# Hybrid mLSTM / attention / gMLP block: which queue starts the projection's stores and the ne rows' spread

## The chip, the cores and the metric

The kernel runs on one core of one Trainium2 chip. The core has five engines, each with a queue of its own that works in order: TensorE (PE; its weight loads are PEld), VectorE (DVE), ScalarE (ACT), GpSimd (POOL) and SyncE (SP). A transfer (DMA) is begun by an instruction in one engine's queue and then runs on the core's 16 DMA engines. The metric is device microseconds of one execution, as the median of several runs; less is better.

## The reference

One layer of a decoder trunk over x (2048 positions, 1024 channels), all in float32. What matters here:

```python
h = rms_norm(x, g_mix) * (1 + scale1) + shift1        # shift, scale, gate from silu(c) @ W_ada + b_ada
p = h @ w_in                                          # one projection for all head groups
y_attn  = forgetting_attention(rms_norm(q_a), rms_norm(k_a), v_a, f_a + b)   # 8 heads x 64
y_mlstm = sigmoid(o_m) * rms_norm(mlstm_chunkwise(q_m, k_m, v_m, i_m, f_m))  # 4 heads x 64
y_sgu   = spatial_gating(gelu(u_s), gelu(v_s))                               # 4 groups x 64
x = x + gate1 * (concat(y_attn, y_mlstm, y_sgu) @ w_out)
x = x + gate2 * conv_ffn(rms_norm(x) * (1 + scale2) + shift2)   # up, causal conv of width 3, SwiGLU, down
```

The mLSTM is a matrix memory with gates in log space. Within a chunk, the weight of source s for target t is exp(a[s] + ne[t]) for s <= t, where a holds one number for each source and head, and ne (the negated running maximum, less the cumulated log gate) one for each target and head.

## The kernel before

Matmuls are exact to about float32: each operand is split into a high and a low part (types F32R), and `mm3` (L53 to L56) makes three products. The work goes through the core in stages: a start that loads x and the first adaptive weights; the projection (here up to about 818 us); attention; the output projection with the second norm; the up projection with the convolution; and the down projection.

**The projection.** `steps` walks over two halves of the sequence and, in each, over twelve column blocks of `w_in` in this order: km with the gates, qm, vm, om, vs, us, then k, v and q of attention, twice. `w_block` loads one block of weights ahead (tile wst, L564), ACT casts its high part (L569) and DVE makes the low part (L570). `natural` makes, for each of eight tiles of 128 positions, 24 matmuls into one of three PSUM banks (`acc`), and a `use_...` function empties the bank and sends the result to DRAM:

- `use_km` (L602): ACT copies, then the tile goes to km_d (L605). `do_qm` (L609): ACT scales, then qm_d (L619). `use_vm` and `use_om` do likewise, but what they send was last written by DVE or POOL.
- `spatial` (L661): four tiles of 128 positions together; ACT copies the transposed result, then yt_d (L679).
- `use_qk` (L692): ACT squares the bank (tile ev, L694), DVE sums, POOL takes the root (L132), DVE scales into qn (L700), which frees the bank. Four tiles later `turn` transposes qn on PE, ACT makes the high part qhi (L710), DVE the low part qlo (L711), and both are sent to q_d or k_d (L713). qhi and qlo share three buffers.

**Beside it.** `mod_sum` makes the rest of the adaptive vectors on DVE (L422, L424) from tiles wa of 256 KB that are loaded through four buffers (L414); `columns_or_row` sends the two gates' rows to gt_d (L468).

**The mLSTM** runs as a background generator, `mlstm(qi)`, for each 512 positions, a piece of which is put between two tiles of the projection. It writes four rows ne to DRAM (ne_d, L799). For each of four chunks of 128 positions, `raw` transposes k on PE, copies it on ACT (kT, L836), and loads into tile M1 (two buffers) the chunk's four ne rows, spread over all 128 partitions by the transfer itself (L838: 512 pieces of 512 bytes, 256 KB, read from the same 2 KB of DRAM). POOL adds the causal mask (L839). `decay` turns M1 into weights with four exponentials on ACT (L845). Then PE makes the scores, DVE multiplies them by M1 (sc, L868), which frees M1's buffer, and the state is brought forward. At the end ACT copies the transposed result and it goes to yt_d (L933).

**Order.** Each engine's queue is in order. The order within a queue isn't that of the program text: a planner (the list scheduler of the tile framework) plays the program through with modelled durations and puts each instruction, transfers included, into its engine's queue when its inputs are ready and its buffers free; among ready ones the earlier in the program goes first. Waits are put in afterwards. Before the change every transfer is begun by SP, which does nothing else.

Of the kernel before, what the change touches and what calls it, by code (L numbers as in the profile page):

```python
# [17 lines left out]
P = 128  # L18
# [6 lines left out]
TB = 512  # L25
# [8 lines left out]
def trunk(  # L34
# [6 lines left out]
    nc = tc.nc  # L41
    V, A, G, T = nc.vector, nc.scalar, nc.gpsimd, nc.tensor
    dma = nc.sync.dma_start
    x, out = x[0], out[0]
    w_ada, w_in, w_out, w_up, w_down = w_ada[0], w_in[0], w_out[0], w_up[0], w_down[0]

    def bc(ap, axis, n):
        u = ap.unsqueeze(axis)
        shape = list(u.shape)
        shape[axis] = n  # L50
        return u.broadcast_to(shape)

    def mm3(ps, lh, ll, rh, rl, start, stop, resume=False):  # L53
        T.matmul(ps, lh, rh, start=start, stop=False, skip_group_check=resume)  # L54
        T.matmul(ps, lh, rl, start=False, stop=False, skip_group_check=resume)  # L55
        T.matmul(ps, ll, rh, start=False, stop=stop, skip_group_check=resume)  # L56
# [9 lines left out]
    ne_d = dr.tile([4, S], F32, name="ne_d")  # L66
    qm_d = dr.tile([2, P, S], F32, name="qm_d")
    km_d = dr.tile([S, 256], F32, name="km_d")
    vm_d = dr.tile([S, 256], F32, name="vm_d")
    om_d = dr.tile([S, 256], F32, name="om_d")  # L70
    yt_d = dr.tile([D, S], F32, name="yt_d")
    y2_d = dr.tile([512, S], F32, name="y2_d")
    x2_d = dr.tile([S, D], F32, name="x2_d")
    gt_d = dr.tile([2, D], F32, name="gt_d")
# [56 lines left out]
    def rsqrt(t, n):  # L131
        G.tensor_tensor(t, t, nhalf[:, 0:1].broadcast_to([P, n]) if n > 8 else nhalf[:, :n], op=ALU.pow)  # L132
# [239 lines left out]
    def acc_ps():  # L372
        n_acc[0] += 1
        return pp.tile([P, 512], F32, name="acc", tag="acc2" if n_acc[0] % 3 == 0 and n_accs[0] == 3 else "acc")

    def tr_ps():
        return pp.tile([P, 512], F32, name="trp", tag="trp")

    def misc_ps():
        return pp.tile([P, 512], F32, name="mp", tag="mp")  # L380

    def mps():
        return pp.tile([P, 512], F32, name="mps", tag="mps")
# [77 lines left out]
    def columns_or_row(acc, col):  # L461
        kind, half = col // 1024, (col % 1024) // 512
        ps = misc_ps()
        if kind in (2, 5):
            T.matmul(ps, ones, acc, start=True, stop=True)
            gr = pool.tile([1, 512], F32, name="gr", tag="t2k")
            A.copy(gr, ps[0:1, :])
            dma(gt_d[kind // 3 : kind // 3 + 1, half * 512 : half * 512 + 512], gr)  # L468
        else:
            for j in range(4):  # L470
                T.matmul(ps[:, j : j + 1], acc[:, j * P : (j + 1) * P], ones[:, 0:1], start=True, stop=True)
            sl = slice(half * 4, half * 4 + 4)
            if kind == 3:
                V.tensor_copy(sh2[:, sl], ps[:, 0:4])
            else:
                V.scalar_tensor_tensor(
                    a2[:, sl], ps[:, 0:4], 1.0, gf[:, half * 4 : half * 4 + 4], op0=ALU.add, op1=ALU.mult
                )
# [123 lines left out]
    def use_km(tt, ps):  # L602
        t = pool.tile([P, 256], F32, name="ev", tag="ev")
        A.copy(t, ps[:, 0:256])
        dma(km_d[tt * P : (tt + 1) * P, :], t)  # L605
        V.tensor_tensor(gates[:, tt, :], ps[:, 256:272], gbias, op=ALU.add)

    def do_qm(half, wb):
        tiles, _ = wb  # L609
        for tb in range(half * 2, half * 2 + 2):  # L610
            for j in range(2):
                ps = acc_ps()
                for k in range(KT):
                    hh, hl = hT[tb, k]
                    wh, wl = tiles[k]
                    mm3(ps, wh[:, j * P : (j + 1) * P], wl[:, j * P : (j + 1) * P], hh, hl, k == 0, k == KT - 1)
                t = pool.tile([P, 512], F32, name="evq", tag="sq")
                A.mul(t, ps, 0.125)
                dma(qm_d[j, :, tb * TB : (tb + 1) * TB], t)  # L619

    def use_vm(tt, ps):
        t = pool.tile([P, 256], F32, name="ev", tag="ev")
# [30 lines left out]
    def use_us(tt, ps):  # L653
        i = tt % 4
        if i == 0:
            sgu["u"] = pool.tile([P, 4, 256], F32, name="su", tag="t4k")
        u, vn = sgu["u"], sgu["v", tt // 4]
        A.activation(u[:, i, :], ps[:, 0:256], AF.Gelu_apprx_tanh)
        if i == 3:
            return lambda: spatial(tt, u, vn)  # L660

    def spatial(tt, u, vn):
        y = pool.tile([P, 4, 256], F32, name="sy", tag="t4k")
        for g in range(4):
            sl = slice(g * 64, g * 64 + 64)
            mp = (misc_ps, tr_ps)[g % 2]()
            m3 = mp[:, 0:256].rearrange("p (n c) -> p n c", n=4)
            T.matmul(m3, wT[:, g, :], vn[:, :, sl], start=True, stop=True)
            V.tensor_tensor(y[:, :, sl], m3, bc(gsgu[:, sl], 1, 4), op=ALU.mult)
            V.scalar_tensor_tensor(  # L670
                y[:, :, sl], y[:, :, sl], bs_col[:, g : g + 1], u[:, :, sl], op0=ALU.add, op1=ALU.mult
            )
        for j in range(2):
            mp = (misc_ps, tr_ps)[j % 2]()
            for n in range(4):
                T.transpose(mp[:, n * P : (n + 1) * P], y[:, n, j * P : (j + 1) * P], ident)
            t5 = pool.tile([P, 512], F32, name="evq", tag="sq")
            A.copy(t5, mp)
            dma(yt_d[768 + j * P : 896 + j * P, (tt - 3) * P : (tt + 1) * P], t5)  # L679

    def use_v(h0):
        def go(tt, ps):
# [8 lines left out]
    def use_qk(which, h0):  # L691
        def go(tt, ps):  # L692
            sq = pool.tile([P, 256], F32, name="ev", tag="ev")
            A.activation(sq, ps[:, 0:256], AF.Square)  # L694
            ss = pool.tile([P, 4], F32, name="ss", tag="ss")
            V.tensor_reduce(ss, sq.rearrange("p (h d) -> p h d", h=4), axis=AX.X, op=ALU.add)
            V.tensor_scalar(ss, ss, 1.0 / 64, EPS, op0=ALU.mult, op1=ALU.add)
            rsqrt(ss, 4)
            n = pool.tile([P, 4, 64], F32, name="qn", tag="q2k")
            V.tensor_tensor(n, ps[:, 0:256].rearrange("p (h d) -> p h d", h=4), bc(ss, 2, 64), op=ALU.mult)  # L700
            return lambda: turn(tt, n)

        def turn(tt, n):
            tp = tr_ps()[:, 0:256]
            for j in range(2):
                T.transpose(tp[:, j * P : (j + 1) * P], n[:, 2 * j : 2 * j + 2].rearrange("p e d -> p (e d)"), ident)
            g, d = (gq8, q_d) if which == "q" else (gk, k_d)
            hi = pool.tile([P, 256], F32R, name="qhi", tag="qhl")
            lo = pool.tile([P, 256], F32R, name="qlo", tag="qhl")
            A.activation(hi, tp, AF.Copy, scale=g)  # L710
            V.scalar_tensor_tensor(lo, tp, g, hi.bitcast(F32), op0=ALU.mult, op1=ALU.subtract)  # L711
            for e, t in enumerate((hi, lo)):
                dma(  # L713
                    d[h0 // 2 : h0 // 2 + 2, e, :, tt * P : (tt + 1) * P].rearrange("h p t -> p h t"),
                    t.bitcast(F32).rearrange("p (h t) -> p h t", h=2),
                )

        return go
# [50 lines left out]
    def mlstm(qi):  # L769
        t0 = qi * 512  # L770
# [8 lines left out]
        m, e, lf = ra[0:4], ra[32:36], ra[64:68]  # L779
# [50 lines left out]
        def raw(n):  # L830

            kps = misc_ps()
            for j in range(2):
                T.transpose(kps[:, j * P : (j + 1) * P], kn[:, n, j * P : (j + 1) * P], ident)
            kT = pool.tile([P, 2, P], F32, name="kT", tag="kT")
            A.copy(kT.rearrange("p a b -> p (a b)"), kps[:, 0:256])  # L836
            M1 = pool.tile([P, 4, P], F32, name="M1", tag="M1")
            dma(M1, ne_d[:, t0 + n * P : t0 + n * P + P].unsqueeze(0).broadcast_to([P, 4, P]))  # L838
            G.tensor_tensor(M1, M1, bc(maskT, 1, 4), op=ALU.add)  # L839
            got[n] = kT, M1  # L840

# [11 lines left out]
        for n in range(4):  # L853
            ch = slice(n * P, n * P + P)
            kT, M1 = got.pop(n)
# [46 lines left out]
            if n < 2:  # L902
                raw(n + 2)
# [23 lines left out]
        for j in range(2):  # L927
            yp = mps()
            for n in range(4):
                T.transpose(yp[:, n * P : (n + 1) * P], hq2[:, n, j * P : (j + 1) * P], ident)  # L930
            yt = pool.tile([P, 512], F32, name="yt", tag="sq")
            A.copy(yt, yp)
            dma(yt_d[512 + j * P : 640 + j * P, t0 : t0 + 512], yt)  # L933

    nat = lambda use: lambda h, w: natural(h, w, use)
    blocks = [
        ([(C_KM, 256), (C_G, 16)], nat(use_km)),
        ([(C_QM, 256)], do_qm),
        ([(C_VM, 256)], nat(use_vm)),
# [676 lines left out]
```

## Time and profile before

| | us |
|---|---|
| median of 3 runs (lowest to highest) | 2716.72 (2711.45 to 2717.74) |
| the profiled execution, its own time | 2712.34 |
| its span, first to last instruction | 2710.6 |
| PE busy | 2586.7 |
| DVE busy | 2005.5 |
| ACT busy | 1305.0 |
| POOL busy | 453.4 |

Rows of a timeline read: start (us from the span's start), duration, engine, line, operation, output <- inputs, count, and in brackets the idle time of the engine just before, with what ended it. Rows of waits read: who waited, for whom; us in total, times, the longest. A row of one line's instructions gives its durations in ns (least, median, greatest) and the first and last start in us. Merged rows (x2, x3) span from the first start to the last end. SPq is SP's queue; issuing a transfer isn't counted as busy time. The profile leaves numbers out of tile names, so M1 appears as M, ne_d in its rows as written.

### The profile page before, as it was taken

Reading aid. Unit: us, or ns where it says so; the run is one execution under the profiler, and the core shown is the slowest. Engines: PE = TensorE matmul, PEld = TensorE weight load, DVE = VectorE, ACT = ScalarE, POOL = GpSimd, SP = SyncE. Lnnn points to the kernel's source line nnn. Section 1 sums busy time; section 2 is a strip of 40 time slices with the busy share of each in tenths; the row PEclk is TensorE's granted clock in tenths of the full one; section 3 lists DMA queues with packets and bytes.
Section 4 is the critical chain, followed back from the end, with each engine's and each line's share of the span. In section 5 each row is a group of like instructions: output and inputs, shape, how many; then the busy total and the mean of one; then the engine's idle time right before and its main releaser. Section 6 shows DMA issues by size and latency. Waiting matters only on the chain.

```text
span 2710.6 us, 40295 instructions
## 1 busy us (share of the span) xinstructions
PE 2586.7 (95%) x14345; PEld 2218.3 (82%) x14345; DVE 2005.5 (74%) x3499; ACT 1305.0 (48%) x2452; POOL 453.4 (17%) x592
## 2 busy tenths in 40 slices
PE   6989899989899999999998999999999999999999
PEld 5988788989897877777786888888888888888787
DVE  7455466245457888885659988887988887898797
ACT  4243235243237887884436544444444444444443
POOL 2022222032335665651000000000000000000000
PEclk9989999999999999999999999999999999999999
DMA  7534465324356454525752322227222225849533
GB/s 251 170 89 145 120 186 178 108 52 148 92 144 170 110 142 117 166 63 190 263 206 70 103 82 87 78 86 287 94 85 80 86 79 180 293 135 312 172 104 117
DMA packets 313085, 382.09 MB, mean 141 GB/s; under 512 B 31004, under 2 KB 214264, under 8 KB 310836
## 3 DMA queue, kind: packets, MB, share of 16 engines
q1 hardware_dynamic: 312884, 379.52, 44.3%
q8 instruction: 113, 1.85, 0.3%
q14 instruction: 88, 0.72, 0.1%
HBM read 278.67 MB, written 100.77 MB: 140 GB/s over the span
## 4 chain that ended last, share of the span: by engine, by line
PE 57%; DVE 5%; ACT 2%; DMA 2%; issue 2%; POOL 1%; SPq 0%; DVEq 0%; ACTq 0%; POOLq 0%
PE ub L56 10%; PE ub L54 10%; PE ub L55 10%; PE db L55 4%; PE db L56 4%; PE db L54 4%; PE tp L263 3%; PE sp L210 3%; PE op L249 2%; PE wps L56 2%; PE wps L55 2%; PE wps L54 2%; PE op L250 2%; DVE wspl L1360 1%; ACT L L227 1%
## 5 line engine op out<-in xcount | busy, mean ns | idle before, releaser
L54 PE MATMUL acc<-whi,hh 128*128 128x256 f32 (+1 forms) x1408 | 419.6, 299 | 27.8 <-DVE qn L700 16.9
L56 PE MATMUL acc<-whi,hl 128*128 128x256 f32 (+1 forms) x1408 | 408.7, 292 | 0.1
L55 PE MATMUL acc<-wlo,hh 128*128 128x256 f32 (+1 forms) x1408 | 408.4, 291 | 0.0
L54 PEld LDWEIGHTS acc<-whi,hh 128*128 128x128 f32 x1408 | 278.9, 198 | 34.3 <-ACT ev L694 9.2
L54 PE MATMUL ub<-T,wsph 128*128 128x512 f32 x704 | 274.2, 390 | 5.8 <-ACT wsph L1228 5.8
L55 PEld LDWEIGHTS acc<-wlo,hh 128*128 128x128 f32 x1408 | 278.9, 198 | 0.5 <-issue 0.2
L56 PEld LDWEIGHTS acc<-whi,hl 128*128 128x128 f32 x1408 | 277.8, 198 | 1.0 <-DVE hl L548 0.7
L56 PE MATMUL ub<-T,wspl 128*128 128x512 f32 x704 | 273.7, 389 | 0.4 <-DVE wspl L1229 0.4
L55 PE MATMUL ub<-T,wsph 128*128 128x512 f32 x704 | 273.9, 389 | 0.0
L55 PE MATMUL db<-wspl,wsph 128*128 128x512 f32 x616 | 240.3, 390 | 2.7 <-DVE wspl L1360 2.7
L56 PE MATMUL db<-wsph,wspl 128*128 128x512 f32 x616 | 239.6, 389 | 0.0
L54 PE MATMUL db<-wsph 128*128 128x512 f32 x616 | 238.3, 389 | 0.3 <-ACT wsph L1359 0.3
L1228 ACT CAST wsph<-S 128x512 fp32r<-128x512 f32 x176 | 109.6, 623 | 229.4 <-PE ub L55 164.1
L267 DVE TENSOR_TENSOR plo<-tp,phi 128x512 fp32r<-128x512 f32 (+1 forms) x320 | 187.1, 607 | 34.2 <-ACT phi L266 32.0
L54 PE MATMUL ub<-B,wsph 128*128 128x512 f32 x528 | 207.2, 392 | 2.8 <-ACT wsph L1228 2.8
L56 PE MATMUL ub<-B,wspl 128*128 128x512 f32 x528 | 207.0, 392 | 0.7 <-DVE wspl L1229 0.7
L55 PE MATMUL ub<-B,wsph 128*128 128x512 f32 x528 | 207.1, 392 | 0.0
L227 ACT ACTIVATE L<-L,nm 128x1024 f32<-128x1024 f32 (+2 forms) x192 | 172.4, 902 | 33.0 <-DVE nm L216 30.3
L263 PE MATMUL tp<-ident,L 128*128 128x128 f32 x1088 | 179.6, 277 | 3.9 <-POOL L L232 1.2
L266 ACT CAST phi<-tp 128x512 fp32r<-128x512 f32 (+1 forms) x320 | 160.6, 521 | 44.2 <-PE tp L263 42.9
L210 PE MATMUL sp<-kk,q 128*128 128x512 f32 (+3 forms) x640 | 169.1, 375 | 2.6 <-DVE nm L216 1.6
L232 POOL TENSOR_SCALAR L<-L,rs 128x1024 f32<-128x1024 f32 (+2 forms) x192 | 167.3, 881 | 11.2
(334 smaller groups left out, 5897.5 us busy)
## 6 DMA issues: line engine op xcount, KB each, us to landing
w<-in_w_up_dram SPq DMA_DIRECT2D x88, 512.0 KB
wd<-in_w_down_dram SPq DMA_DIRECT2D x176, 256.0 KB
wa<-in_w_ada_dram SPq DMA_DIRECT2D x96, 256.0 KB
wst<-in_w_in_dram SPq DMA_DIRECT2D x48, 512.0 KB
act_d<-yc SPq DMA_DIRECT2D x44, 512.0 KB
act<-act_d SPq DMA_DIRECT2D x44, 512.0 KB
q<-q_d SPq DMA_DIRECT2D x128, 128.0 KB
hc_d<-hl SPq DMA_DIRECT2D x28, 512.0 KB
```

The costliest lines, as they stand in the source:

```text
L54: T.matmul(ps, lh, rh, start=start, stop=False, skip_group_check=resume)
L55: T.matmul(ps, lh, rl, start=False, stop=False, skip_group_check=resume)
L56: T.matmul(ps, ll, rh, start=False, stop=stop, skip_group_check=resume)
L210: T.matmul(sp[:, b : b + bw], q2[n][:, qs], kk[:, s0 + b : s0 + b + bw], start=n == 0, stop=n == 1 and not last)
L227: A.activation(L[c], L[c], AF.Exp, bias=nm[:, n - 1 : n], scale=-1.0, accum_out=rs[:, c : c + 1])
L232: G.tensor_scalar(t, t, rs[:, 0:1], 1.0, op0=ALU.mult, op1=ALU.mult)
L249: T.matmul(op[:, c0:], vv[:, j, :], hi[:, c0:], start=(j == 0), stop=False)
L250: T.matmul(op[:, c0:], vv[:, j, :], lo[:, c0:], start=False, stop=(j == ns - 1))
L263: T.transpose(tp[:, i * P : (i + 1) * P], rows[i][j // 8][:, (j % 8) * P : (j % 8 + 1) * P], ident)
L266: A.copy(hi[:, c0:], tp[:, c0:])
L267: V.tensor_tensor(lo[:, c0:], tp[:, c0:], hi[:, c0:].bitcast(F32), op=ALU.subtract)
L1228: A.copy(hi, src)
```

## The change

Some transfers are begun from ACT's queue (`nc.scalar.dma_start`) in place of SP's: the stores of what ACT has just written in the projection (gate rows, km, qm, the two yt stores, and qhi of each qhi/qlo pair) and the load that spreads the ne rows into M1. Everything else stays with SP: weights, x, the adaptive weights, qlo, v, vm, om, ne_d itself, and all transfers of the later stages. No transfer changes its size or shape, and nothing computed changes.

```diff
     dma = nc.sync.dma_start
+
+    dma_a = nc.scalar.dma_start
@@ columns_or_row
             A.copy(gr, ps[0:1, :])
-            dma(gt_d[kind // 3 : kind // 3 + 1, half * 512 : half * 512 + 512], gr)
+            dma_a(gt_d[kind // 3 : kind // 3 + 1, half * 512 : half * 512 + 512], gr)
@@ use_km
         A.copy(t, ps[:, 0:256])
-        dma(km_d[tt * P : (tt + 1) * P, :], t)
+        dma_a(km_d[tt * P : (tt + 1) * P, :], t)
@@ do_qm
                 A.mul(t, ps, 0.125)
-                dma(qm_d[j, :, tb * TB : (tb + 1) * TB], t)
+                dma_a(qm_d[j, :, tb * TB : (tb + 1) * TB], t)
@@ spatial
             A.copy(t5, mp)
-            dma(yt_d[768 + j * P : 896 + j * P, (tt - 3) * P : (tt + 1) * P], t5)
+            dma_a(yt_d[768 + j * P : 896 + j * P, (tt - 3) * P : (tt + 1) * P], t5)
@@ use_qk, turn
             for e, t in enumerate((hi, lo)):
-                dma(
+                (dma_a, dma)[e](
                     d[h0 // 2 : h0 // 2 + 2, e, :, tt * P : (tt + 1) * P].rearrange("h p t -> p h t"),
                     t.bitcast(F32).rearrange("p (h t) -> p h t", h=2),
                 )
@@ mlstm, raw
             M1 = pool.tile([P, 4, P], F32, name="M1", tag="M1")
-            dma(M1, ne_d[:, t0 + n * P : t0 + n * P + P].unsqueeze(0).broadcast_to([P, 4, P]))
+            dma_a(M1, ne_d[:, t0 + n * P : t0 + n * P + P].unsqueeze(0).broadcast_to([P, 4, P]))
             G.tensor_tensor(M1, M1, bc(maskT, 1, 4), op=ALU.add)
@@ mlstm, end
             A.copy(yt, yp)
-            dma(yt_d[512 + j * P : 640 + j * P, t0 : t0 + 512], yt)
+            dma_a(yt_d[512 + j * P : 640 + j * P, t0 : t0 + 512], yt)
```

## The prediction

> **What bounds the kernel now.** I read the page first, then busy time by stage, then what TensorE waited for in the stage that the change touches, then the spread of the ne rows (the tile is M1 in the code; the profile drops the number and calls it M).
>
> ```profile
> span 2710.6 us, 40295 instructions
> PE 2586.7 (95%) x14345; PEld 2218.3 (82%) x14345; DVE 2005.5 (74%) x3499; ACT 1305.0 (48%) x2452; POOL 453.4 (17%) x592
> ...
> 50.00:815.00 765.00, 700.81 (x5347) 670.84 (x5346) 395.58 (x932) 272.54 (x525) 180.47 (x179) 0.96 0.45 129
> ```
>
> The window columns are length, then busy time with instruction count of PE, PEld, DVE, ACT and POOL, then granted clock, DMA share and GB/s. TensorE sets the end. Every transfer that moves is issued between 50 and 818 us, so only the projection can change: 64 us in which PE is not busy, and a granted clock of 0.96, which is worth another 0.04 x 765 = 31 us. Nothing moved belongs to the stages behind it. ACT is busy for 273 of 765 us.
>
> What PE waited for in that window (us in total, times, longest), and below it what ACT and SP's queue waited for:
>
> ```profile
> PE acc L54 <- DVE qn L700: 16.9, 9, 8.4
> PE trp L706 <- DVE qlo L711: 8.7, 3, 4.5
> PE mp L668 <- ACT kT L836: 7.3, 2, 4.0
> ...
> ACT ev L694 <- PE acc L56: 100.0, 43, 5.3
> ACT M L845 <- POOL M L839: 65.7, 13, 8.6
> ...
> SPq L713 <- ACT qhi L710: 67.4, 36, 15.5
> SPq L838 <- DVE sc L868: 48.2, 7, 26.3
> ```
>
> PE never waits for a moved store. It waits for evictions (qn, qlo, kT) that stand behind ACT, and ACT's second largest wait is for the masked ne rows. One such wait in full, every engine:
>
> ```profile
> 328.27 0.37 SPq L838 DMA_DIRECT2D M<-ne_d  x1
> 328.68 0.50 SPq L414 DMA_DIRECT2D wa<-in_w_ada_dram  x1
> 337.39 1.26 POOL L839 TENSOR_TENSOR M<-M,maskT 128x512 f32<-128x512 f32 x1 [8.39 <-DMA M<-ne_d]
> 338.69 1.28 ACT L845 ACTIVATE M<-M,acol 128x128 f32<-128x128 f32 x4 [8.63 <-POOL M L839]
> 337.96 0.98 DVE L422 TENSOR_SCALAR modacc<-wa,cs 128x512 f32<-128x512 f32 x1 [7.74 <-DMA wa<-in_w_ada_dram]
> 341.23 0.66 PE L706 MATMUL trp<-ident,qn 128*128 128x128 f32 x2 [4.54 <-DVE qlo L711]
> ```
>
> The spread takes 337.39 - 328.27 = 9.1 us from issue to use. ACT stands still for 8.63 us and PE loses 4.54 of them: an ACT stall costs PE itself less about 4 us of cover. The wa load issued 0.4 us behind the spread lands at the same moment, so on this queue what follows a spread waits for it, and DVE stands 7.74 us for that.
>
> **The change part by part.** *Issues that leave SP for ACT.* 64 qhi stores, 16 spreads, 16 km, 8 qm, 8 + 8 yt and 4 gate rows: 124.
>
> ```profile
> L713 SPq DMA_DIRECT2D k_d<-qhi x32: 359/374/1890, 262.3 to 767.4; - x32
> L713 SPq DMA_DIRECT2D q_d<-qhi x32: 359/372/831, 329.7 to 817.2; - x32
> L838 SPq DMA_DIRECT2D M<-ne_d x16: 359/378/638, 162.5 to 726.1; - x16
> L605 SPq DMA_DIRECT2D km_d<-ev x16: 319/336/497, 52.7 to 476.1; - x16
> ```
>
> On SP one issue takes 0.34 to 0.38 us (median): 64 x 0.373 + 16 x 0.378 + 16 x 0.336 + 28 others at about 0.33 = 44.5 us. No ACT issue is in this trace. The lower bound is nothing, if ACT's queue issues under the previous operation's tail; the upper is 44.5 us of ACT time. Most of it is hidden by ACT's own waiting: 100.0 / 43 = 2.3 us of idle ahead of each qk eviction, six times an issue. It shows where ACT is already late and PE behind it: one issue after eight of ACT's 13 stalls for M, the share that I count as felt by PE (8 x 0.37 = 3.0), two at the tail of the last q block (0.7), three km stores where ACT also squares the second block of x (1.0). I take 4.7 us; uncovered entirely it would be 44.5.
>
> *SP's waits go, and its queue runs ahead.* The 48.2 us at L838 and 67.4 at L713 no longer hold up loads. Where does a late load reach PE? Two places:
>
> ```profile
> 162.49 0.98 SPq L838 DMA_DIRECT2D M<-ne_d  x2
> 167.94 0.35 SPq L414 DMA_DIRECT2D wa<-in_w_ada_dram  x1
> 173.70 1.27 POOL L839 TENSOR_TENSOR M<-M,maskT 128x512 f32<-128x512 f32 x1 [1.12 <-DMA M<-ne_d]
> 174.26 1.25 DVE L424 SCALAR_TENSOR_TENSOR modacc<-wa,cs,modacc 128x512 f32<-128x512 f32 x1 [3.73 <-DMA wa<-in_w_ada_dram]
> 178.84 0.54 PE L834 MATMUL mp<-ident,kn 128*128 128x128 f32 x2 [4.71 <-DVE sh L474]
> ...
> 195.64 0.38 SPq L838 DMA_DIRECT2D M<-ne_d  x1
> 197.56 0.33 SPq L414 DMA_DIRECT2D wa<-in_w_ada_dram  x1
> 210.99 0.34 SPq L414 DMA_DIRECT2D wa<-in_w_ada_dram  x1
> 213.87 0.75 DVE L424 SCALAR_TENSOR_TENSOR modacc<-wa,cs,modacc 128x512 f32<-128x512 f32 x1 [2.91 <-DMA wa<-in_w_ada_dram]
> 215.69 0.38 SPq L838 DMA_DIRECT2D M<-ne_d  x1
> 225.13 1.26 POOL L839 TENSOR_TENSOR M<-M,maskT 128x512 f32<-128x512 f32 x1 [15.72 <-DMA M<-ne_d]
> 229.43 0.70 PE L668 MATMUL mp<-sv,wT 128*128 128x256 f32 x2 [4.00 <-ACT kT L836]
> ```
>
> First, the wa of 167.94 lands just behind the second spread; on a queue without spreads it would need 213.87 - 210.99 = 2.9 us and be there at 170.8, so DVE's 3.73 us go and PE's gap of 4.71 shrinks by up to as much: I take 3.0. Second, DVE's 2.91 us at 213.87 delay the spread of 215.69, since it waits for sc behind them on DVE; without them PE's 4.00 us gap shrinks by up to 2.9: I take 1.5, half, because ACT may be late by itself. At 341 PE gains nothing from an earlier wa: ACT stands there anyway.
>
> *The spread itself.* It could be issued earlier only where SP held it up after its buffer was free:
>
> ```profile
> 352.71 0.42 DVE L868 TENSOR_TENSOR sc<-mps,M 128x256 f32<-128x256 f32 x1
> 355.42 0.46 SPq L838 DMA_DIRECT2D M<-ne_d  x1
> 364.97 1.28 ACT L845 ACTIVATE M<-M,acol 128x128 f32<-128x128 f32 x4 [7.81 <-POOL M L839]
> 366.51 0.35 PE L54 MATMUL acc<-whi,hh 128*128 128x256 f32 x1 [2.16 <-ACT ev L694]
> ```
>
> Here 355.42 - 353.13 = 2.3 us; at 328.27 and 215.69 SP issues it at once. ACT reaches it in its own order, behind evictions, so I take 1.0 of 2.16. Its flight stays: it is as long alone (9.1) as with wa loads right behind it (225.13 - 215.69 = 9.4). The Trainium skill, DMA: Bandwidth & Descriptors, section "Issuing engines are not separate DMA queues", says that transfers from different issuers run on the same DMA engines and interleave, and that several issuers save only the issue time; by that rule the 5.5 us gained here would be 0, and the sum +5.7 us. Its section "Queues, rings and completion order" has each DMA engine alternate between the issuers' rings packet by packet, which would let the wa past the spread, as I assume. No row here has two issuers and can decide.
>
> That the loads now share the DMA engines with the spread costs the spread something. Between nothing and the whole load time beside it (below, 11.8 us over all), I take 1.0 us, near nothing, from 9.1 against 9.4.
>
> *Sum.* +4.7 - 3.0 - 1.5 - 1.0 + 1.0 = +0.2 us on the profiled execution's 2712.34, which lies 4.4 us under the runs' median of 2716.72. So 2717 us on the median's scale.
>
> *Order.* A planner sets each engine's order from modelled times, so 124 issues on ACT can swap neighbours there. Its price lies in the same gaps, either way.
>
> **The rivals.** *Faster, 2705 us.* All three gaps close (3.7 + 2.9 + 2.2 = 8.8), a tenth of the 31 us of lost clock comes back with the gaps (3), and ACT's issues are hidden: 2716.7 - 12. For it: DVE's and SP's waits above. Against: most of PE's loss is the spread's own flight.
>
> *Slower, 2729 us: ACT takes over SP's wait for sc.* On ACT that wait holds every eviction behind it. SP's longest is 26.3 us (to 328.2). If the spread stands ahead of one eviction on ACT, ACT waits about a third to a half of it there, 8 to 14 us; less the 4 us of cover PE loses 4 to 10, and with two or three such places 12 us. It decides from the point where sc comes over 4 us after ACT gets there. Against it: ACT reaches the place later than SP, in step with DVE.
>
> *Slower, 2728 us: the spread loses its queue to itself.* At 297 the loads that stood behind it now run beside it:
>
> ```profile
> 297.18 0.98 SPq L838 DMA_DIRECT2D M<-ne_d  x2
> 298.80 3.06 SPq L564 DMA_DIRECT2D wst<-in_w_in_dram  x2
> 311.47 1.26 POOL L839 TENSOR_TENSOR M<-M,maskT 128x512 f32<-128x512 f32 x1 [3.73 <-DMA M<-ne_d]
> 315.45 0.55 PE L54 MATMUL acc<-whi,hh 128*128 128x256 f32 x1 [8.38 <-DVE qn L700]
> ```
>
> A wst load is 512 KB, a wa load 256 KB; at the 2.9 us of a lone wa for either, as an estimate, two wst here (5.9), one in the second half (2.9) and three wa at 1 us are 11.8 us that go straight into PE's gaps. For it: PE follows ACT there.
>
> **How the numbers follow.** Forecast (about 2717, no change that can be told) 0.47, its own range 2709 to 2725; faster 0.28; the two slower ones 0.13 and 0.12. What a measurement of this kernel can tell from no change is about 0.3%, 8 us. Predicted 2717; the range takes in both sides' cases and some of the unknown order: 2700 to 2733. Faster 0.28, same 0.47, slower 0.25.
>
> **What would show it.** Right: projection still ends near 818 us; DVE's waits for wa fall well below the present ones at 174 and 338; spreads still need 8 to 10 us and ACT still waits about 66 us for M. Wrong towards faster: PE's gaps at 178 and 229 gone and nothing new. Wrong towards slower: ACT waiting on its queue for sc, or spreads of 11 us and more beside loads. If wa still lands with the spread, the queues are not apart.

## The result, and the profile after

The changed kernel takes 2731.45 us (median of 6 runs, 2726.36 to 2735.36), the kernel before 2717.50 us beside it. The ratio is 1.0053, with a 95% interval of 1.0037 to 1.0069: slower by 14 us, more than the 0.3% that can be told from no change. The forecast of no change fails; the time lies inside the range, 1.5 us under its upper end.

The profiled execution took 2731.69 us, and its span of 2730.0 us is 19.4 us longer than before. The last matmul of the projection ends at 827.8 us (809.3 before), so the projection holds 18.5 of them. Its window in the changed kernel; the columns are length, busy time with count of PE, PEld, DVE, ACT and POOL, then granted clock, DMA share and GB/s:

```profile
50.00:834.00 784.00, 706.03 (x5348) 675.29 (x5347) 392.46 (x931) 271.70 (x523) 182.01 (x180) 0.95 0.43 126
```

It is 19 us longer than the window that ended at 815. TensorE is not busy for 784.00 - 706.03 = 78.0 us of it, against 64.2: 13.8 us of new gaps. It is busy 706.03 - 700.81 = 5.2 us longer with the same matmuls, at a granted clock of 0.95 for 0.96.

What TensorE, ACT and DVE waited for in that window of the changed kernel (us in total, times, longest). Line numbers are two higher than before: L642 was L640, L696 was L694, L841 was L839.

```profile
PE acc L56 <- ACT ev L642: 15.5, 5, 8.6
PE acc L56 <- DVE qn L702: 10.9, 6, 3.8
...
PE acc L56 <- ACT ev L696: 8.3, 1, 8.3
...
ACT L810 <- DMA ne_d<-rb: 10.1, 1, 10.1
...
DVE modacc L426 <- DMA wa<-in_w_ada_dram: 45.7, 24, 7.6
DVE modacc L424 <- DMA wa<-in_w_ada_dram: 10.8, 5, 4.9
```

And the rows of the kernel before that answer to the two evictions and to DVE's loads:

```profile
PE acc L54 <- ACT ev L640: 6.3, 4, 2.2
...
PE acc L54 <- ACT ev L694: 2.2, 1, 2.2
...
DVE modacc L424 <- DMA wa<-in_w_ada_dram: 38.9, 19, 7.8
DVE modacc L422 <- DMA wa<-in_w_ada_dram: 17.8, 6, 7.7
```

Three things are to be seen. TensorE's waits moved from DVE (qn, 16.9 before) to ACT's evictions: L642 grew from 6.3 to 15.5 us, L696 from 2.2 to 8.3. ACT has a wait that it did not have, for the landing of the ne rows, 10.1 us. And DVE's waits for wa did not fall: 45.7 + 10.8 = 56.5 us after, 56.7 before.

The largest new gap can be followed from end to end. The changed kernel around it, ACT first, then POOL and DVE, then TensorE:

```profile
572.84 0.38 ACT L642 ACTIVATE ev<-acc 128x256 f32<-128x256 f32 x1 [10.65 <-DVE sv L653]
572.87 0.94 ACTq L840 DMA_DIRECT2D M<-ne_d  x2
588.21 1.28 ACT L847 ACT_TABLE_LOAD   x1 [8.29 <-DVE acol L812]
...
581.27 1.30 POOL L841 TENSOR_TENSOR M<-M,maskT 128x512 f32<-128x512 f32 x1 [3.95 <-DMA M<-ne_d]
584.95 1.26 POOL L841 TENSOR_TENSOR M<-M,maskT 128x512 f32<-128x512 f32 x1 [1.81 <-DMA M<-ne_d]
586.17 1.01 POOL L134 TENSOR_TENSOR mu<-mu,nhalf 128x4 f32<-128x4 f32 x1
587.22 0.83 DVE L653 TENSOR_TENSOR sv<-ev,mu 128x256 f32<-128x256 f32 x1 [3.42 <-POOL mu L134]
591.65 0.58 PE L56 MATMUL acc<-whi,hh 128*128 128x256 f32 x1 [8.59 <-ACT ev L642]
```

The same place in the kernel before:

```profile
562.38 0.92 SPq L838 DMA_DIRECT2D M<-ne_d  x2
...
565.46 0.38 ACT L640 ACTIVATE ev<-acc 128x256 f32<-128x256 f32 x1 [10.64 <-DVE sv L651]
570.76 1.29 POOL L839 TENSOR_TENSOR M<-M,maskT 128x512 f32<-128x512 f32 x1 [2.71 <-DMA M<-ne_d]
573.87 1.27 POOL L839 TENSOR_TENSOR M<-M,maskT 128x512 f32<-128x512 f32 x1 [0.26 <-DMA M<-ne_d]
574.36 0.39 PE L54 MATMUL acc<-whi,hh 128*128 128x256 f32 x1 [2.24 <-ACT ev L640]
575.25 1.01 POOL L132 TENSOR_TENSOR mu<-mu,nhalf 128x4 f32<-128x4 f32 x1
...
580.73 0.39 PE L54 MATMUL acc<-whi,hh 128*128 128x256 f32 x1 [1.51 <-ACT ev L640]
```

Before, SP had begun these two spreads at 562.4, while ACT stood for sv. Now they stand in ACT's queue behind that eviction, and begin 0.03 us after it, at 572.87. That is 4.5 us behind the store of the ne rows (568.35), where SP began them 1.4 us behind it (560.98). By the eviction the whole stage is 572.84 - 565.46 = 7.4 us later than before; the first addition of the mask on POOL is 10.5 us later and the second 11.1. POOL works in order, and in both kernels a step L134 (L132 before), which sv needs, stands behind both additions: at 575.25 before, at 586.17 now. DVE's sv waits for it and acol stands behind sv, ACT waits 8.29 us for acol, with the next eviction of TensorE's sums behind that, and TensorE starts at 591.65 in place of 580.73, 10.9 us later. So 3.5 us are lost here. The gap of 8.59 us takes the place of two, 2.24 and 1.51: the L134 of the tile before stood between the two additions (572.01) and now stands ahead of them (576.32), so that this tile no longer waits.

A gap costs a second time. Two windows of the changed kernel behind it:

```profile
592.00:597.00 5.00, 5.00 (x27) 5.00 (x27) 4.12 (x9) 4.97 (x9) 2.79 (x2) 0.56 0.30 87
597.00:603.00 6.00, 6.00 (x53) 5.79 (x53) 3.01 (x10) 5.49 (x10) 2.17 (x3) 1.00 0.36 106
```

For 5 us TensorE is busy at a granted clock of 0.56 and does 5.4 matmuls per us, afterwards 8.8. The Trainium skill, TensorE: Matmul & The Clock Gate, section "HAM oscillation — how this bites in real kernels", describes the same: a pause of more than some 3.4 us lets the gate halve the clock for the work behind it. The trace agrees for this gap. The trace of the kernel before has the clock fall behind a shorter one too, the 2.24 us above, where the granted clock is 0.50 for the 3.3 us from 575.10 on:

```profile
575.10:578.40 3.30, 3.30 (x18) 3.30 (x17) 1.90 (x6) 1.12 (x1) 2.42 (x5) 0.50 0.00 0
```

The second new gap, 8.31 us, has another cause. The changed kernel, and below it the kernel before:

```profile
695.21 0.38 ACTq L840 DMA_DIRECT2D M<-ne_d  x1
709.79 1.26 POOL L841 TENSOR_TENSOR M<-M,maskT 128x512 f32<-128x512 f32 x1 [4.64 <-DMA M<-ne_d]
711.58 1.01 POOL L134 TENSOR_TENSOR ss<-ss,nhalf 128x4 f32<-128x4 f32 x1
713.20 0.55 PE L56 MATMUL acc<-whi,hh 128*128 128x256 f32 x1 [8.31 <-ACT ev L696]
...
682.44 1.07 SPq L838 DMA_DIRECT2D M<-ne_d  x2
692.44 1.01 POOL L132 TENSOR_TENSOR ss<-ss,nhalf 128x4 f32<-128x4 f32 x1
695.48 1.28 POOL L839 TENSOR_TENSOR M<-M,maskT 128x512 f32<-128x512 f32 x1 [1.44 <-DMA M<-ne_d]
```

By the store of the ne rows (693.81 for 679.82) the stage is 14.0 us late here. The first spread begins 12.8 us later than before, so it lost nothing on ACT, and the second addition, 14.3 us later, is in step. But the planner has put POOL's queue in another order: the step L134 that stood between the two additions stands behind both now and comes 19.1 us later, some 5 us behind the stage, and with it the scaling into qn that frees a bank of TensorE's sums.

### The profile page after: what moved, and what is told of

It is laid out like the page before. It is cut to its first block, busy times and chain, and to the rows that moved or that the text cites. A ratio compares the mean times of both kernels' runs of the same rounds, so it can differ in the third digit from the quotient of the medians.

```text
span 2730.0 us, 40208 instructions
## 1 busy us (share of the span) xinstructions
PE 2590.6 (95%) x14345; PEld 2221.3 (81%) x14345; DVE 2002.8 (73%) x3499; ACT 1303.4 (48%) x2450; POOL 455.4 (17%) x592
## 4 chain that ended last, share of the span: by engine, by line
PE 60%; DVE 7%; DMA 3%; ACT 2%; issue 2%; POOL 1%; SPq 0%; ACTq 0%; DVEq 0%; POOLq 0%
PE ub L58 10%; PE ub L56 10%; PE ub L57 10%; PE db L57 4%; PE db L58 4%; PE db L56 4%; PE tp L265 3%; PE sp L212 3%; PE op L251 2%; PE wps L58 2%; PE wps L57 2%; PE wps L56 2%; PE op L252 2%; DVE wspl L1362 1%; DMA M<-ne_d 1%
## 5 line engine op out<-in xcount | busy, mean ns | idle before, releaser
L56 PE MATMUL acc<-whi,hh 128*128 128x256 f32 (+1 forms) x1408 | 421.7, 300 | 42.5 <-ACT ev L642 15.5
L234 POOL TENSOR_SCALAR L<-L,rs 128x1024 f32<-128x1024 f32 (+2 forms) x192 | 167.2, 881 | 11.2
```

The lines of the kernel that those rows point to most:

```text
L234: G.tensor_scalar(t, t, rs[:, 0:1], 1.0, op0=ALU.mult, op1=ALU.mult)
```

## The experiments

The effect of each kernel is its ratio to the kernel before, timed beside it on the same chip (medians 2717 to 2720 us), less 1, times 2720 us. The intervals of the ratios are 0.1 to 0.17% wide to either side, 3 to 5 us.

**Which part of the change costs.** Four kernels move parts of the 124 transfers.

```
e1: all stores                        dma_a(...) -> dma(...)     spread stays on ACT
e2: the spread, L840                  dma_a(M1, ...) -> dma(M1, ...)   stores stay on ACT
e3: only the high halves of q and k   (dma_a, dma)[e]            all else on SP
e4: only km, qm, yt and gate rows     dma_a(...)                 all else on SP
```

Only the spread on ACT:

> Only the spread of the ne rows (16 transfers) is begun from ACT; the stores are all back on SP. Theory A, the spread is the whole loss (ACT stands at it until the ne rows have landed, 10.1 us in one row of the changed kernel, and issues it behind its own evictions): 2728 to 2734 us, the projection's last matmul near 827, the wait on the ne rows again in ACT's rows. Theory B, the 108 stores are the loss (their issue time and what their new places do to ACT's order and to shared buffers): 2714 to 2720 us, last matmul near 809, and the ACT wait on the ne rows, if it is there, costs PE nothing. Theory C, no move by itself but the new order of all queues: something between, 2721 to 2727, and e1 and e2 together do not add up to the +14.

All the stores on ACT:

> All 108 stores are begun from ACT as in the changed kernel, the spread is back on SP. Theory A (the spread): 2714 to 2720 us, no wait of ACT on the ne rows, and the PE gaps of 8.6 and 8.3 us in the first step after each half-way point fall back to those of before. Theory B (the stores): 2728 to 2734 us, and the projection's step of q in the first half is still about 4 us late behind ACT's wait for the store of yt. Theory C: 2721 to 2727.

Only the stores of the high halves:

> Only the 64 stores of the high halves of q and k are begun from ACT; the small stores and the spread are on SP. Theory A: 2714 to 2720 us. Theory B, by issue time: 64 of 124 issues of 0.37 us are 23 us of ACT, and if these cost PE in proportion, 2723 to 2727. If SP's waits on the low halves were what held the loads, the time falls below 2714, since half of the issues that SP makes in these steps are gone.

Only the small stores:

> Only the small stores are begun from ACT (km, qm, both kinds of yt, the gate rows: 44 transfers); the halves of q and k and the spread are on SP. Theory A: 2714 to 2720 us. Theory B, by shared buffers: the squares of the next half's norm wait for the store of yt, PE loses about 4 us at 417 to 440 us as in the changed kernel, 2720 to 2725. A store that starts sooner because SP no longer has other waits ahead of it should free its buffer sooner: then below 2715.

| on ACT | transfers | us | ratio | 95% interval | effect, us |
|---|---|---|---|---|---|
| all | 124 | 2731.45 | 1.0053 | 1.0037 to 1.0069 | +14 |
| spread (e1) | 16 | 2728.62 | 1.0034 | 1.0022 to 1.0047 | +9 |
| all stores (e2) | 108 | 2726.24 | 1.0025 | 1.0015 to 1.0034 | +7 |
| high halves (e3) | 64 | 2726.24 | 1.0027 | 1.0016 to 1.0039 | +7 |
| small stores (e4) | 44 | 2720.76 | 1.0005 | 0.9996 to 1.0015 | +1, not told from 0 |

Neither theory A (the spread is all) nor B (the stores are all) holds: the spread costs 9 us, the stores 7, and 9 + 7 agrees with 14 within the intervals. So the sum gives no support to theory C, that the parts do not add up. But the new order of the queues, of which it speaks, does have a share: the gap of 8.3 us at 713 us comes with the spread alone too (8.2 below). The stores' cost is that of the high halves. The wait of ACT's squares for the store of yt, which the expectations speak of, is no cause that can be told from nothing: with the small stores alone the time does not move.

The traits of the spread come and go with it. What TensorE waited for in the projection with only the spread on ACT:

```profile
PE acc L56 <- ACT ev L642: 13.6, 4, 7.0
...
PE acc L56 <- ACT ev L696: 8.2, 1, 8.2
```

and with all stores on ACT and the spread on SP:

```profile
PE acc L56 <- ACT ev L642: 8.2, 4, 3.7
```

**How far two profiles of one kernel differ.**

> The kernel before once more, unchanged, for a second profile of it. The profiled execution of before (span 2710.6 us) lay at the fast end of its timed runs. If its gaps on TensorE (60.0 us between 50 us and the projection's end, 17 us of them behind the normalised q and k) are those of this kernel, they come again within 2 us; if executions differ by more than that, differences of a few us between the profiles of one kernel and the next mean nothing, and only the timed runs do.

```profile
50.00:813.00 763.00, 694.87 (x5346) 665.14 (x5345) 395.88 (x931) 272.74 (x525) 180.60 (x178) 0.97 0.45 130
```

The span came again, 2710.5 us. The projection's gaps were 763.00 - 694.87 = 68.1 us against 64.2, more than the 2 us expected. Its TensorE is also busy 5.9 us less, with a clock of 0.97. So differences of under 4 us in gaps, or 6 us in busy time, between two profiles of different kernels are not read here, and the 13.8 and 5.2 us above become 78.0 - 68.1 = 9.9 us of gaps and 706.03 - 694.87 = 11.2 us of busy time against this profile: their sum, 19 and 21, is firmer than the split. Both profiles of the kernel before lie at the fast end of its runs (2712 us, median 2717 to 2720), which is why the spans differ by 19 us and the timed medians by 14.

**ACT's stand for the ne rows.** In this run the first spread of each four goes back to SP.

> As the run with only the spread on ACT, but the first of the four spreads of each 512 positions (4 of 16 transfers), the one that follows the store of the ne rows, stays on SP. Theory A1, ACT stands at the first spread until the ne rows have landed and that is the loss: 2717 to 2722 us, no wait of ACT for the ne rows. Theory A2, the loss is that spreads stand in ACT's order behind its evictions and exponentials, at all four chunks: 2725 to 2730 us, with 3 of 4 of them still there.

```
- dma_a(M1, ne_d[...])
+ (dma if n == 0 else dma_a)(M1, ne_d[...])
```

It took 2731.22 us, ratio 1.0046 (1.0033 to 1.0060), +13 us: not less than with all 16 on ACT. But it does not take the stand away: its ACT waits 10.2 us for the ne rows. The second spread of the four reads the same rows and follows at once, so ACT waits for them there. The run says that freeing the first spread alone brings nothing; it decides nothing on the stand.

**The flight of the spread.** The two kernels that follow keep the ne rows in DRAM by chunk, so that each of the 128 partitions reads one piece of 2 KB in place of four of 512 bytes. The bytes are the same, and each engine's order of instructions is that of the kernel that they start from.

```
- ne_d = dr.tile([4, S], F32, name="ne_d")
+ ne_d = dr.tile([S // P, 512], F32, name="ne_d")
- dma(ne_d[:, t0 : t0 + 512], ne)
+ dma(ne_d[qi * 4 : qi * 4 + 4, :].rearrange("n (h l) -> h n l", l=P), r4(ne))
- dma(M1, ne_d[:, t0 + n * P : t0 + n * P + P].unsqueeze(0).broadcast_to([P, 4, P]))
+ dma(M1.rearrange("p h l -> p (h l)"), ne_d[qi * 4 + n : qi * 4 + n + 1, :].broadcast_to([P, 512]))
```

The kernel before with this layout:

> The kernel before, with the ne rows kept in DRAM by chunk, so that one spread reads 128 pieces of 2 KB in place of 512 pieces of 512 bytes; every engine's order of instructions stays. Theory, the spread's flight of 8 to 9 us is set by its pieces and is what POOL, then DVE and ACT and then TensorE stand for: flight 3 to 5 us (a plain load of 256 KB took 2.9 us), gaps on TensorE some 5 to 15 us fewer, 2705 to 2715 us. Rival, the flight is set by the one place in DRAM that all 128 partitions read, or nobody on the way to TensorE waits for it: flight still 8 us or time still 2716 to 2722 us.

The changed kernel with it:

> The changed kernel, with the ne rows kept by chunk as in the run before this one (every engine's order as in the changed kernel). If what the spread on ACT costs is the lateness of its landing, a shorter flight gives most of it back: 2718 to 2725 us. If the cost is ACT standing for the store of the ne rows, or the issue time of the stores, the flight does not matter for it: the gain is at most that of the run with the spread on SP, 2724 to 2732 us.

| kernel | us | ratio to the kernel before | 95% interval |
|---|---|---|---|
| before, 2 KB pieces | 2666.57 | 0.9809 | 0.9792 to 0.9825 |
| changed, 2 KB pieces | 2675.35 | 0.9840 | 0.9825 to 0.9855 |

The first is 52 us faster where 2 to 12 were expected, and beats both kernels. One spread in the kernel before with 512-byte pieces (its issue, at 195.64, is shown in the prediction) and then with 2 KB pieces:

```profile
204.79 1.29 POOL L839 TENSOR_TENSOR M<-M,maskT 128x512 f32<-128x512 f32 x1 [6.79 <-DMA M<-ne_d]
```

```profile
193.94 0.33 SPq L840 DMA_DIRECT2D M<-ne_d  x1
197.06 1.28 POOL L841 TENSOR_TENSOR M<-M,maskT 128x512 f32<-128x512 f32 x1 [0.75 <-DMA M<-ne_d]
```

The projection's window with 2 KB pieces:

```profile
50.00:771.00 721.00, 684.14 (x5353) 655.84 (x5352) 397.90 (x933) 273.23 (x525) 183.18 (x180) 0.99 0.46 138
```

From issue to use the spread takes 204.79 - 195.64 = 9.1 us in the one and 197.06 - 193.94 = 3.1 us in the other. The projection's gaps fall from 64.2 to 36.9 us, the longest wait for qn from 8.4 to 1.9, and the clock rises from 0.96 to 0.99, which takes 700.81 - 684.14 = 16.7 us off TensorE's busy time. That is the second price of a gap again, and why 27 us of gaps were worth 44. Against the second profile of the kernel before, it is 68.1 - 36.9 = 31 us of gaps and 10.7 us of busy time, 42 in all. The expectation left the clock out.

The changed kernel still loses 0.0031, 8 us, to the unchanged one when both read 2 KB pieces. The two kernels below split that.

> Only the spread is begun from ACT, and the ne rows are kept by chunk, so that the spread reads 2 KB pieces; every engine's order is that of the run with only the spread on ACT. That run cost +9 us with 512-byte pieces. Theory A2, the cost is that ACT begins the spread late and POOL, DVE, ACT and TensorE then stand for a landing that is on the path: with a flight of 3 to 4 us most landings are early enough, so the cost falls to 0 to 4 us over the kernel with 2 KB pieces and all on SP: 2664 to 2671 us. Rival, ACT's own stand at the spread (for the ne rows, for the buffer) costs TensorE whatever the flight: +7 to +11, 2673 to 2678 us.

> Only the 64 stores of the high halves are begun from ACT, and the ne rows are kept by chunk; every engine's order is that of the run with these stores alone, which cost +7 us. Theory D, the stores cost ACT's issue time (64 of 0.37 us, 24 us on the engine that evicts TensorE's sums): the cost does not hang on the spread, 2671 to 2676 us. Rival, it was the spread again, which the changed order put later: 0 to 3 us, 2664 to 2670 us.

Spread on ACT: 2669.51 us, ratio 0.9821 (0.9806 to 0.9837), which is 3 us over 0.9809. High halves on ACT: 2670.17 us, 0.9828 (0.9813 to 0.9843), 5 us over. The first lies where theory A2 (late landings) expects it and not where ACT's own stand would put it, and ACT's stand is all there in it: it waits 10.1 us for the ne rows, once, as with 512-byte pieces.

At the first place followed above, this kernel, with the same late issue:

```profile
537.19 0.38 ACT L642 ACTIVATE ev<-acc 128x256 f32<-128x256 f32 x1 [10.65 <-DVE sv L653]
537.22 0.81 ACTq L840 DMA_DIRECT2D M<-ne_d  x2
541.64 1.30 POOL L841 TENSOR_TENSOR M<-M,maskT 128x512 f32<-128x512 f32 x1
544.50 1.30 POOL L841 TENSOR_TENSOR M<-M,maskT 128x512 f32<-128x512 f32 x1
551.38 0.58 PE L56 MATMUL acc<-whi,hh 128*128 128x256 f32 x1 [3.96 <-ACT ev L642]
```

POOL finds both spreads landed, and TensorE stands 3.96 us, where it stood 7.0 with the spread alone on ACT and 512-byte pieces (2.5 with all on SP and 2 KB). At the second place the step L134 still stands behind both additions (655.88, behind 651.95 and 654.05), and no gap of TensorE over 1.5 us follows. So the late start and the new order of POOL became gaps because the landing was on the path.

The windows from 50 us to the projection's last matmul, first with 512-byte and then with 2 KB pieces, the spread alone on ACT in both:

```profile
50.00:822.20 772.20, 699.42 (x5342) 670.94 (x5340) 392.13 (x923) 267.93 (x518) 176.92 (x174) 0.95 0.44 128
50.00:762.80 712.80, 679.39 (x5341) 652.02 (x5340) 395.24 (x923) 268.67 (x517) 178.65 (x174) 0.99 0.46 138
```

The gaps are 72.8 and 33.4 us. With all on SP they are 60.0 and 63.9 (two profiles) with 512-byte pieces and 32.9 with 2 KB. So the spread on ACT adds 9 to 13 us of gaps with 512-byte pieces, more than the 4 us by which two profiles differ, and 0.5 us with 2 KB. The timed medians go the same way, from +9 to +3, but not beyond their intervals (+9 is 6 to 13, +3 has 6 us to either side). The result for the high halves lies between the two theories' numbers and decides nothing.

**The issue time of the stores.** Each store of a high half is made two, one for each head; 512-byte ne rows as at first, all else on SP.

> As the run with the 64 stores of the high halves on ACT (512-byte ne rows as before), but each of them in two transfers, one for each head: 128 issues on ACT in place of 64, the same bytes. Theory D (issue time on ACT): some 24 us more of ACT, and at the rate of the single stores (7 us for 24 us) +5 to +9 more, 2730 to 2736 us. Rival, the place in the order and not the time: within 3 us of the single stores, 2723 to 2729 us.

```
- (dma_a, dma)[e](d[h0 // 2 : h0 // 2 + 2, e, :, ...], t...)      # for hi
+ for j in range(2):
+     dma_a(d[h0 // 2 + j, 0, :, ...], hi.bitcast(F32)[:, j * P : (j + 1) * P])
```

2732.41 us, ratio 1.0056 (1.0042 to 1.0069), +15 us. The issues on ACT (shortest, median and longest in ns), first with 64, then with 128:

```profile
L715 ACTq DMA_DIRECT2D k_d<-qhi x32: 366/366/454, 264.0 to 776.7; - x32
L715 ACTq DMA_DIRECT2D q_d<-qhi x32: 366/366/734, 332.3 to 826.8; - x32
...
L715 ACTq DMA_DIRECT2D k_d<-qhi x64: 326/395/1431, 265.6 to 780.4; - x64
L715 ACTq DMA_DIRECT2D q_d<-qhi x64: 326/342/1307, 334.1 to 833.0; - x64
```

Sums over all issues are 24.4 and 53.8 us. The cost goes from 7 to 15 us with them: 0.3 us for each us that ACT issues. That is theory D's number, for the high halves, and not yet its cause, for the places were not followed one by one. The wait of TensorE for qn, 17 us in both profiles of the kernel before, does not follow the cost: it is 18.8 us with 64 issues and 24.3 with 128, but 21.2 with the small stores alone, which cost nothing that can be told. And one thing is not separated from the issue time: with 128 issues ACT's copies of v (L687) stand 7.3 us for stores of k that have not landed, a wait that they do not have with 64.

The 44 small stores would cost 4 us at the same rate (14.5 us of issues); measured is +1, with an interval from -1 to +4. So the rate is not shown for them.

**POOL's stand, with 2 KB pieces.** The last kernel moves the line that adds the mask (L841) from the start of the transfer to the exponentials that use it.

> All transfers on SP, the ne rows kept by chunk, and POOL's addition of the mask to a spread stands one stage later in the recurrence, next to the exponentials that need it, instead of right behind the start of the transfer; only POOL's order differs from that of the run with 2 KB pieces. If POOL, which works in order, still stands for landings with work of the evictions behind it, TensorE's gaps fall further below the 32.9 us of that run and the time is 2652 to 2663 us. If with 2 KB pieces the landings cost nothing more, 2663 to 2670 us; if the exponentials now wait for the later addition, 2670 to 2680 us.

2665.85 us, ratio 0.9800 (0.9786 to 0.9813), against 0.9809 with the line in its old place. But the planner, and not the program text, sets the order, and it put the addition where it was: at 542.18 us it stands between the steps L134 of 540.63 and 543.76, as it stood at 542.84 between those of 541.29 and 544.41, and the instructions of POOL, ACT, DVE and SP follow each other as before. So the run says nothing on POOL's place for the addition; that stays untested. It is a second timing of the kernel with 2 KB pieces and all on SP. Against this one the spread on ACT costs 6 us in place of 3, the high halves 8 in place of 5, and both 11 in place of 8, so what 2 KB pieces save on the spread's price is shown by the gaps more than by the times.

## Why the prediction was right in its range and wrong in its steps

That the time lies in the range is owed to the range's width: it took in the cases of both sides, while the sum had +0.2 us and came out 14 us short.

*The bound.* Right in kind: TensorE sets the end, only the projection changed, and its gaps and clock are what moved. "Most of PE's loss is the spread's own flight" stood there only as an argument against the faster rival. The layout of 2 KB pieces shows it and more: 27 to 31 us of gaps, and 11 to 17 us through the clock.

*"SP's waits go, and its queue runs ahead"* (-3.0 and -1.5) is the first step that failed. It had a wa load pass the spread on another queue. The changed kernel has the case, a spread from ACT and two wa loads from SP beside it from 218.9 on, and below it the spread of the last paragraph of this section:

```profile
215.56 0.37 ACTq L840 DMA_DIRECT2D M<-ne_d  x1
218.91 0.80 SPq L416 DMA_DIRECT2D wa<-in_w_ada_dram  x2
224.67 1.26 POOL L841 TENSOR_TENSOR M<-M,maskT 128x512 f32<-128x512 f32 x1 [12.81 <-DMA M<-ne_d]
226.51 1.54 DVE L426 SCALAR_TENSOR_TENSOR modacc<-wa,cs,modacc 128x512 f32<-128x512 f32 x2 [7.55 <-DMA wa<-in_w_ada_dram]
...
328.14 0.37 ACTq L840 DMA_DIRECT2D M<-ne_d  x1
```

DVE starts on the loads 226.51 - 218.91 = 7.6 us after their issue, 1.8 us behind the spread's use; in the kernel before, on the spread's own queue, the same loads took 7.9 us (218.25 to 226.12), and a load without a spread ahead of it took 2.9 in the prediction. That is the sign which the prediction named: "If wa still lands with the spread, the queues are not apart". The rule of the Trainium skill (DMA: Bandwidth & Descriptors, "Issuing engines are not separate DMA queues") agrees with this row, and would have put the sum at +5.7 us. TensorE's two gaps that were to shrink, 4.71 us at 178.8 and 4.00 at 229.4, have 4.18 us at 175.2 and 2.84 and 3.34 us at 226.7 and 232.0 in their place.

*"The spread itself"* (-1.0) had the wrong sign and is the largest miss, +9 us. At 355 the spread did start earlier as said, at 352.54 for 355.42, but TensorE's gap of 2.16 us behind it has 2.25 and 2.59 us in its place. And the step looked for places where SP was late and took from "ACT reaches it in its own order, behind evictions" only that the gain is small. At 565 SP was early and ACT was the late one, by that very order, and 3.5 us were lost. That the flight stays was right: 8 to 10 us alone.

*"Order"* had no term in the sum, since "Its price lies in the same gaps, either way", and it spoke of neighbours on ACT. At 711 us it was POOL's queue that changed, with the start of the spread no later, and 4 to 5 us were lost by it. What else the move costs was not followed place by place.

*"Issues that leave SP for ACT"* was sized too low: 4.7 us taken for all 124, 7 us measured for the stores. The high halves cost 0.3 of their issue time, against the 4.7 / 44.5 = 0.1 assumed; that it is the issue time that costs is argued by the doubled issues and not shown.

*Sharing the DMA engines* (+1.0): nothing contradicts it, and the slower rival built on it ("the spread loses its queue to itself") did not come: no longer flights for single spreads. But 9.1 us, which the prediction gives as the flight of a spread alone, is that of one with a wa load 0.4 us behind it; the spread of 355.42, with no load of weights begun behind it until it landed, took 363.67 - 355.42 = 8.3 us.

*The slower rival "ACT takes over SP's wait for sc"*, 2729 us, was closest in time and right in kind, and wrong in its wait. ACT has no wait for sc of that size; where SP had waited longest for it (328.27), ACT began the spread at 328.14. What ACT put ahead of the spread was its own eviction, and that one's wait for sv. It also did not name the 10.1 us that ACT stands for the ne rows. With 2 KB pieces that stand is still there, and the whole move of the spread costs 3 to 6 us (6 to either side).

## What to carry to other kernels

Before a transfer is moved to another engine's queue, read what stands ahead of it there and what that waits for: the transfer inherits that wait, and if its landing is on the path the gap costs once as idle time and again as clock. Then read the other engines' queues in the new trace too, for a planner that knows of the move may put their work in another order, and check that an edit meant to move an instruction has moved it. Shorten the flight before moving its start: reading one piece for each partition in place of four took 52 us off this kernel, where moving its start cost 9. Transfers begun from a busy engine take issue time there, 0.37 us each here; 64 of them cost this kernel 7 us and 128 cost 15, three tenths of that time.

## What the runs showed of the hardware

A spread of the same 2 KB to 128 partitions, 256 KB in all, took 9.1 us in 512 pieces of 512 bytes (from four rows in DRAM) and 3.1 us in 128 pieces of 2 KB (from one), a factor of 2.9. The Trainium skill, DMA: Bandwidth & Descriptors, section "Why small descriptors are slow (HBM only)", gives a fixed overhead of about 3 cycles for each packet beside one cycle for 32 bytes. As an estimate by that page, a piece of 512 bytes would take 19 cycles and one of 2 KB 67, so the change of layout would save 1 - 67 / (4 x 19) = 12%. The measurement differs and decides; that all partitions read one place is not slow by itself, for the 2 KB pieces do so too, and a plain load of 256 KB took 2.9 us. Whether pieces of 512 bytes cost that much only when they read the same places stays open: no run had pieces of 512 bytes from a place of their own for each partition.
